# Rope scores over stacked parts, forgetting attention by key block, and separate key and query scales

## The chip, the cores and the metric

The kernel runs on one core of a Trainium2 chip. The metric is the device time of one execution in microseconds (us). Before the change three runs gave 2504.44, 2506.77 and 2509.23 us, median 2506.77. The chip's engines are called by what they do here: TensorE (PE in the rows; its weight loads are PEld), VectorE (DVE), ScalarE (ACT), GpSimd (POOL) and SyncE (SP), which issues the DMAs.

## The reference, cut to what matters

The program computes three transformer blocks over 512 tokens and 1024 features, all in float32. The change touches two attentions. The first is the latent attention of the second block: 8 heads, a query and key of 192 features each, of which 128 carry no position and 64 go through rope; the rope part of the key is one for all heads.

```python
q = (rms_norm(q_lat, q_a_norm) @ w_uq).reshape(B, S, 8, 192)
kv = (rms_norm(kv_lat, kv_a_norm) @ w_ukv).reshape(B, S, 8, 128 + 128)
k = concatenate([k_nope, k_pe], -1)          # k_pe: the same 64 for every head
q = rms_norm(q, q_head_norm); k = rms_norm(k, k_head_norm)
q = concatenate([q[..., :128], rope(q[..., 128:])], -1)   # and k the same
o = causal_softmax_attention(q, k, v, 1 / sqrt(192))
```

The second is the forgetting attention of the third block: 8 heads of 64 features, with a running sum of log forget gates as bias.

```python
for blk in range(4):                          # 128 queries each
    logits = q[q0:q1] @ k[:q1].T * scale + cum[q0:q1, None] - cum[None, :q1]
    p = softmax(where(causal, logits, NEG_INF))
    outs.append(p @ v[:q1])
```

## The kernel before, in words

Everything is held with features (or keys) on the 128 partitions and 512 tokens along the free dimension. A projection splits both operands into a high and a low fp32r part and adds three matmuls (`mm`, lines 429 to 431, 512 columns each; `mm_tok`, lines 439 to 441, 256 columns). Weights come by DMA, 512 KB each, through three raw buffers, are split by ScalarE (line 419) and VectorE (line 420) and lie in two pools of six buffers, `whp` for the high and `wlp` for the low parts. A pool `t` has 53 buffers of 128x512 fp32, and `q` has three for values that live for a few instructions. Of the eight PSUM banks three go to projections (`pm`), two to scores (`sc`), and one each to the roles `tr` (transposes), `po` (value products) and `ms` (everything small: column sums, broadcasts, rope's swap).

The program is written as one list of instructions, and a planner orders them on each engine by priority (the order in which they are written) among those that its own cost model takes to be ready; tiles get a buffer when one is free. So the order on each engine is fixed before the run, and instructions of neighbouring pieces are mixed. `self.fillers` is a list of functions (projections that nobody needs yet), of which one is written after every softmax step by `self.fill()`. `self.later(f, depth)` puts a function in a queue and runs the oldest when more than `depth` are waiting; `flush()` runs the rest, with one filler between two.

Latent attention (`mla`) works on four pairs of heads. For a pair, `kv` makes keys and values and the keys' sums of squares; `q` makes three query tiles (the last has the rope parts of both heads, 64 rows each), their sums of squares into the same PSUM tile, and the rope; `scales` turns all 16 columns of sums into scales with one power on GpSimd (line 572); `keys` broadcasts the keys' scales over partitions (line 1287 in two halves of 64 rows for the rope part, line 584 over 128 rows for each head) and multiplies. The work of the next pair is given as fillers to the loop of the present one. In the loop each head goes through its four query blocks, the widest first: a 128-row fp32 matmul (line 1326), a 64-row fp32 matmul for the rope part (line 1327), the mask (line 1328, bf16), then maximum, exponential and normalization; `apply` transposes the probabilities and multiplies them with the values (line 1304), two steps later.

Forgetting attention (`fox_pair`) also takes pairs of heads, with 64 rows (and 64 output columns) each. Scores of both heads (line 1712) and masks (line 1714) come first, then the softmax; `apply`, one step later, turns the block of each head (line 947, into the one `tr` bank, copied by ScalarE at line 949) and adds the value products by query block and key block (line 1701), 128 columns each:

```python
aT = [self.transposed(p, qb) for p in ps]
for kb in range(qb + 1):
    for par, r in enumerate(ROWS):
        nc.tensor.matmul(po[0][r, qb * P:P * (qb + 1)], vt[...], aT[par][:, kb * P:(kb + 1) * P], start=kb == 0, stop=kb == qb)
```

During the first two pairs the fillers are the other branch's values and the second group's projections, during the last two the other branch's outputs (with a gelu of four VectorE and ScalarE steps each) and four `out_a` projections of twelve matmuls each, which need that branch's norm. After the last pair come `flush()`, `branch_rstd(nb)` (column sums and a power), what is left of the fillers, and `branch("gn_b", ...)`, whose results the next projections need.

Of the kernel before, what the change touches and what calls it, by code (L numbers as in the profile page):

```python
# [286 lines left out]
class Net:  # L287
# [902 lines left out]
    def mla(self, norm, third):  # L1190
# [31 lines left out]
        mulc, addc = self.const([P, 16], F32, "mulc"), self.const([P, 16], F32, "addc")  # L1222
        for j in range(NB):
            kc, qc = slice(4 * j, 4 * j + 2), slice(4 * j + 2, 4 * j + 4)
            nc.vector.memset(mulc[:, kc], 1.0 / 192)
            nc.vector.memset(mulc[:, qc], 1.0)
            nc.vector.tensor_scalar(addc[:, kc], kcol[:, j:j + 1].to_broadcast([P, 2]), 1.0 / 192, EPS, mult, add)
            nc.vector.tensor_scalar(addc[:, qc], vq[:, j:j + 1].to_broadcast([P, 2]), 192 * EPS, None, mult)
# [10 lines left out]
        def pair(c):  # L1239
# [3 lines left out]
            def kv():  # L1243
                w = self.load("w_ukv", c, 1, 512)
                r["sums"], r["k"], r["q"], r["v"] = self.psa("sums"), [], [], []
                for par in range(2):
                    ps = self.psm()
                    self.mm(ps, w, par * P, kvs)
                    y = self.t(F32, "kn")
                    nc.scalar.copy(y, ps)  # L1250
                    sq = self.q(F32, "sq")
                    nc.scalar.activation(sq, ps, AF.Square)
                    self.sums(r["sums"], sq, par, 1, par == 0)
                    r["k"].append(y)
                for tp in range(2):
                    ps = self.psm()
                    for b in range(2):
                        self.mm_tok(ps[:, b * 256:(b + 1) * 256], kvs, 2 * tp + b, w, 256, 256)
                    y = self.t(F32, "mv")
                    nc.vector.tensor_copy(y, ps)  # L1260
                    r["v"].append(y)

            def q():
                w = self.load("w_uq", c, 2, 384)
                for i in (2, 0, 1):
# [6 lines left out]
                    self.sums(r["sums"], sq, 2 + i % 2, 1 + i // 2, False, i < 2)  # L1272
                    r["q"].append(y)
                r["qr"] = self.rope(r["q"].pop(0), self.v("qh_r"), cos, sin)

            def scales():
                m = self.s(16, "ms")
                nc.vector.tensor_tensor(m, r["sums"][:, 0:16], mulc, mult)
                nc.vector.tensor_tensor(m, m, addc, add)
                r["rs"] = self.rpow(m, 16)  # L1280
# [12 lines left out]

            return [kv, q, scales, keys], r
# [18 lines left out]
        for f in (work[0], gates[1], work[1], work[2], gates[2], work[3]):  # L1313
            f()
        for c in range(4):
# [5 lines left out]
            for par in range(2):  # L1321
                rp = slice(64 * par, 64 * par + 64)
                for qb in range(NB - 1, -1, -1):
# [3 lines left out]
                    nc.tensor.matmul(ps[:, :n], cur["qr"][rp, qb * P:n], cur["kr"][rp, :n], start=False, stop=False)  # L1327
# [3 lines left out]
                    sc = cur["rs"][:, 4 * qb + 2 + par:4 * qb + 3 + par]  # L1331
# [357 lines left out]
    def fox_pair(self, q, k, vt, c, cl, cum, out, norm):  # L1689
        nc = self.nc  # L1690
        mult, add = ALU.mult, ALU.add
        po = []

        def apply(ps, qb):
            if not po:
                po.append(self.psa("fxo", "po"))
            aT = [self.transposed(p, qb) for p in ps]
            for kb in range(qb + 1):
                for par, r in enumerate(ROWS):
                    col = (kb % 2) * 256 + (2 * cl + par) * 64  # L1700
                    nc.tensor.matmul(po[0][r, qb * P:P * (qb + 1)], vt[kb // 2][:, col:col + 64], aT[par][:, kb * P:(kb + 1) * P], start=kb == 0, stop=kb == qb)  # L1701
            if qb == 0:
                y = self.t(F32, "fxo")
                nc.vector.tensor_copy(y, po[0])
                out.append(y)
                norm.add(c, y)

        for qb in range(NB - 1, -1, -1):
# [6 lines left out]
            prob = []  # L1715
            for par, ps in enumerate(sc):
                cb = cum[2 * c + par]
                p = self.t(F32, "fxp")
                mx = self.s(4, "mx")
                nc.vector.tensor_tensor_reduce(p[:, :n], ps[:, :n], cb[:, :n], 1.0, 4 * NEG, add, ALU.max, mx[:, 0:1])  # L1720
                nc.vector.tensor_scalar(mx[:, 1:2], mx[:, 0:1], -1.0, None, mult)
                self.last = nc.scalar.activation(p[:, :n], p[:, :n], AF.Exp, bias=mx[:, 1:2], scale=1.0, accum_out=mx[:, 2:3])
                nc.vector.reciprocal(mx[:, 3:4], mx[:, 2:3])
                nc.vector.tensor_scalar(p[:, :n], p[:, :n], mx[:, 3:4], None, mult)
                prob.append(p)
            self.fill()
            self.later(lambda p=prob, qb=qb: apply(p, qb), 1)
# [52 lines left out]
```

## Time and profile before

| what | value |
|---|---|
| runs | 2504.44, 2506.77, 2509.23 us |
| the profiled execution | 2498.9 us, its span 2497.1 us, 31348 instructions |
| mean granted clock of TensorE | 0.988 |
| TensorE busy | 2438.4 us, 98% of the span |
| TensorE weight loads busy | 1994.1 us, 80% |
| VectorE, ScalarE, GpSimd busy | 1313.5, 983.0, 62.7 us |
| projections, lines 429, 430, 431 | 2736 each, 1045.1, 1042.8 and 1040.7 us busy |
| latent attention's scores | about 1274 to 1424 us from the span's start |
| forgetting attention | about 1900 to 2058 us |

Busy time of TensorE counts a matmul from its start to the modelled end of its pipeline, so neighbours overlap and the sum of their durations is more than the time that passes. What one costs is read in the timeline as the distance to the next start. In a row with a count (x4) the length runs from the first start to the last end. A clock of 0.50 is 1.2 GHz, 1.00 is 2.4 GHz.

### The profile page before, as it was taken

What the parts mean: (1) busy time and instruction counts of PE and PEld (TensorE: products, weight loads), DVE (VectorE), ACT (ScalarE), POOL (GpSimd) and SP (SyncE); (2) the same over time, 40 slices, a digit from 0 to 9 for tenths busy, and PEclk for the clock granted to TensorE, in tenths of its full rate; (3) what the DMA queues carried; (4) which work ended last, traced back from release to release, by engine and by line L of the source; (5) the groups of instructions that cost most, each with busy time, mean ns of one, the idle gap of its engine ahead of it and who ended that gap; (6) DMA issues with size and microseconds to landing.
All of it is one profiled execution on the core that took longest, in us unless ns stands there. A gap on an engine that the chain in (4) does not pass through costs nothing. (4 is left out here: it accounts for less than half of the span.)

```text
span 2497.1 us, 31348 instructions
## 1 busy us (share of the span) xinstructions
PE 2438.4 (98%) x12622; PEld 1994.1 (80%) x12622; DVE 1313.5 (53%) x2220; ACT 983.0 (39%) x1575; POOL 62.7 (3%) x62
## 2 busy tenths in 40 slices
PE   8999999999999999999999999999999999999998
PEld 6877788888888787777877798888898768888887
DVE  7536556774775664446555654223365465432333
ACT  5423433442444445655324533222245344322221
POOL 0000000000000000000000000000010001000001
PEclk9999999999999999999999999999999989999999
DMA  5223225433433332222322113233213101323321
GB/s 188 93 90 101 90 97 185 135 123 114 152 119 119 126 109 77 68 81 83 113 71 85 37 66 118 93 101 101 93 54 103 61 26 60 96 93 101 100 87 49
DMA packets 71746, 240.78 MB, mean 96 GB/s; under 512 B 8232, under 2 KB 11184, under 8 KB 71600
## 3 DMA queue, kind: packets, MB, share of 16 engines
q1 hardware_dynamic: 71600, 238.78, 29.1%
q8 instruction: 99, 1.62, 0.3%
q14 instruction: 47, 0.39, 0.0%
HBM read 236.64 MB, written 2.11 MB: 96 GB/s over the span
## 5 line engine op out<-in xcount | busy, mean ns | idle before, releaser
L429 PE MATMUL pm<-hi,wh 128*128 128x512 f32 (+1 forms) x2736 | 1045.1, 383 | 11.1 <-ACT hi L393 7.3
L430 PE MATMUL pm<-lo,wh 128*128 128x512 f32 (+1 forms) x2736 | 1042.8, 381 | 0.0
L431 PE MATMUL pm<-hi,wl 128*128 128x512 f32 (+1 forms) x2736 | 1040.7, 380 | 0.0
L419 ACT CAST wh<-raw 128x1024 fp32r<-128x1024 f32 (+1 forms) x372 | 382.3, 1029 | 827.0 <-PE pm L430 581.5
L420 DVE TENSOR_TENSOR wl<-raw,wh 128x1024 fp32r<-128x1024 f32 (+1 forms) x372 | 445.0, 1196 | 448.8 <-ACT wh L419 422.2
L429 PEld LDWEIGHTS pm<-hi,wh 128*128 128x128 f32 x2736 | 517.2, 189 | 110.9 <-ACT hi L393 8.9
L430 PEld LDWEIGHTS pm<-lo,wh 128*128 128x128 f32 x2736 | 517.0, 189 | 96.5 <-issue 3.8
L431 PEld LDWEIGHTS pm<-hi,wl 128*128 128x128 f32 x2736 | 516.8, 189 | 96.1 <-issue 3.6
L439 PE MATMUL pm<-wh,hi 128*128 128x256 f32 x400 | 116.0, 290 | 4.9 <-ACT vt L816 4.9
L1393 DVE CUSTOM_DVE_ANT_0 adaw<-adaw,cb 128x1024 f32<-128x1024 f32 x72 | 87.9, 1220 | 55.7 <-DMA adaw<-in_w_ada 55.5
L441 PE MATMUL pm<-wh,lo 128*128 128x256 f32 x400 | 115.1, 288 | 0.0
L440 PE MATMUL pm<-wl,hi 128*128 128x256 f32 x400 | 114.2, 286 | 0.0
L1472 DVE TENSOR_TENSOR sg<-sg,pm 128x512 f32<-128x512 f32 x44 | 30.2, 686 | 132.8 <-PE pm L431 132.7
L572 POOL TENSOR_TENSOR rc<-ms,nhalf 128x4 f32<-128x4 f32 (+2 forms) x29 | 38.6, 1333 | 2335.2 <-DVE ms L577 1779.3
L439 PEld LDWEIGHTS pm<-wh,hi 128*128 128x128 f32 x400 | 77.8, 194 | 5.8 <-ACT vt L816 5.3
L441 PEld LDWEIGHTS pm<-wh,lo 128*128 128x128 f32 x400 | 77.8, 194 | 0.5 <-issue 0.3
L440 PEld LDWEIGHTS pm<-wl,hi 128*128 128x128 f32 x400 | 77.8, 194 | 0.5 <-issue 0.2
L481 PE MATMUL pm<-hi,wh 128*128 128x256 f32 (+1 forms) x216 | 61.5, 309 | 9.9 <-ACT hi L400 7.1
L970 DVE SCALAR_TENSOR_TENSOR uy<-ur,vec,uy 128x511 f32<-128x511 f32 x88 | 65.7, 747 | 9.0 <-ACT uy L968 8.0
L258 DVE TENSOR_TENSOR acc<-acc,sq 128x512 f32<-128x512 f32 (+1 forms) x93 | 54.6, 595 | 24.0 <-ACT sq L254 22.8
L482 PE MATMUL pm<-lo,wh 128*128 128x256 f32 (+1 forms) x216 | 66.0, 307 | 0.3 <-DVE lo L1424 0.3
L483 PE MATMUL pm<-hi,wl 128*128 128x256 f32 (+1 forms) x216 | 66.2, 308 | 0.0
(350 smaller groups left out, 2363.7 us busy)
## 6 DMA issues: line engine op xcount, KB each, us to landing
raw<-in_w_gu SPq DMA_DIRECT2D x88, 512.0 KB, 3.3
adaw<-in_w_ada SPq DMA_DIRECT2D x72, 512.0 KB, 3.3
raw<-in_w_dn SPq DMA_DIRECT2D x48, 512.0 KB, 3.3
raw<-in_w_up SPq DMA_DIRECT2D x44, 512.0 KB, 3.3
raw<-in_w_g SPq DMA_DIRECT2D x16, 512.0 KB, 3.3
raw<-in_w_l0qk SPq DMA_DIRECT2D x16, 512.0 KB, 3.4
raw<-in_w_l SPq DMA_DIRECT2D x12, 512.0 KB, 3.3
X<-in_x SPq DMA_DIRECT2D x16, 256.0 KB, 5.6
```

What stands on the lines that cost most here:

```text
L419: nc.scalar.copy(wh[:, :n], raw[:, :n])
L420: nc.vector.tensor_tensor(wl[:, :n], raw[:, :n], wh[:, :n].bitcast(F32), ALU.subtract)
L429: self.nc.tensor.matmul(out, a, xh, start=start and k == 0, stop=False)
L430: self.nc.tensor.matmul(out, a, xl, start=False, stop=False)
L431: self.pe = self.nc.tensor.matmul(out, b, xh, start=False, stop=stop and k == n - 1)
L439: self.nc.tensor.matmul(out, xh[:, sl], a, start=start and k == 0, stop=False)
L440: self.nc.tensor.matmul(out, xh[:, sl], b, start=False, stop=False)
L441: self.pe = self.nc.tensor.matmul(out, xl[:, sl], a, start=False, stop=stop and k == len(x) - 1)
L482: self.nc.tensor.matmul(o[:, sl], wh[:, k], xl[:, sl], start=False, stop=False)
L483: self.nc.tensor.matmul(o[:, sl], wl[:, k], xh[:, sl], start=False, stop=k == 7)
L970: nc.vector.scalar_tensor_tensor(y[:, sh:], raw[:, :S - sh], self.v("fconv_w", 44 * (2 - sh) + f), y[:, sh:], mult, add)
L1393: nc.vector.tensor_tensor_reduce(w, w, cb, 0.5, 0.0, ALU.mult, ALU.add, mod[:, i:i + 1])
```

## The change

In latent attention the rope part of a query is split into a high and a low fp32r part that are stacked, high in the head's own 64 rows and low in the other 64. The rope part of the key, which has the same 64 features in both halves, is scaled with the broadcast over 128 rows and split into a high and a low tile; these lie in one buffer of `whp` or `wlp` for each head. Line 1327 becomes two one-pass matmuls over 128 rows, one with the key's high and one with its low part. The half-height broadcasts of line 1287 are gone. The function `scales` is gone as a step: the keys' scales are made in `kv`, right behind their sums, the queries' in `q`, each with one VectorE instruction and a power of 8 columns.

In forgetting attention the probabilities of all four query blocks of a pair are kept, in five tiles. Four functions per pair go into the queue and are run one per step of the next pair: three turn the key blocks (0; 1 and 3; 2) of both heads, into the `tr` and `ms` banks in turns, one copy of 512 columns per bank; the fourth, `values`, multiplies by key block, with 512, 384, 256 and 128 columns, and stores the result.

```diff
-        mulc, addc = self.const([P, 16], F32, "mulc"), self.const([P, 16], F32, "addc")
+        addk, addq = self.const([P, 8], F32, "addk"), self.const([P, 8], F32, "addq")
...
+        def scales(ps, f, a):
+            m = self.s(8, "ms")
+            nc.vector.scalar_tensor_tensor(by2(m), ps[:, 0:16].rearrange("p (j c) -> p j c", c=4)[:, :, 0:2], f, by2(a), mult, add)
+            return self.rpow(m, 8)
...
-                    self.sums(r["sums"], sq, par, 1, par == 0)
+                    self.sums(sums, sq, par, 1, par == 0, par == 1)
...
+                r["rk"] = scales(sums, 1.0 / 192, addk)
...
+                r["rq"] = scales(sums, 1.0, addq)
+                qr = self.rope(r["q"].pop(0), self.v("qh_r"), cos, sin)
+                r["qr"] = []
+                for own, other in (ROWS, ROWS[::-1]):
+                    y = self.t(F32R, "qs")
+                    nc.scalar.copy(y[own], qr[own])
+                    nc.vector.tensor_tensor(y[other], qr[own], y[own].bitcast(F32), ALU.subtract)
+                    r["qr"].append(y)
...
             def keys():
-                rs = r["rs"]
-                bk = self.psa("pbc")
-                for j in range(NB):
-                    for par in range(2):
-                        nc.tensor.matmul(bk[64 * par:64 * par + 64, j * P:(j + 1) * P], rs[:, 4 * j + par:4 * j + par + 1].to_broadcast([P, 64]), self.ident, start=True, stop=True)
-                r["kr"] = self.t(F32, "krc")
-                nc.vector.tensor_tensor(r["kr"], kr, bk, mult)
+                rk = r["rk"]
+                r["kr"] = []
                 for par in range(2):
-                    b = self.bcast_ps([rs[:, 4 * j + par:4 * j + par + 1] for j in range(NB)])
+                    b = self.bcast_ps([rk[:, 2 * j + par:2 * j + par + 1] for j in range(NB)])
                     nc.vector.scalar_tensor_tensor(r["k"][par], r["k"][par], gqk, b, mult, mult)
+                    y = self.q(F32, "krc")
+                    nc.vector.tensor_tensor(y, kr, b, mult)
+                    w = (self.whp, self.wlp)[par].tile([P, 1024], F32R, tag=("wh", "wl")[par], name="krs")
+                    h, l = w[:, 0:S], w[:, S:2 * S]
+                    nc.scalar.copy(h, y)
+                    nc.vector.tensor_tensor(l, y, h.bitcast(F32), ALU.subtract)
+                    r["kr"].append((h, l))
-            return [kv, q, scales, keys], r
+            return [kv, q, keys], r
...
-                    nc.tensor.matmul(ps[:, :n], cur["qr"][rp, qb * P:n], cur["kr"][rp, :n], start=False, stop=False)
+                    for kr_part in cur["kr"][par]:
+                        nc.tensor.matmul(ps[:, :n], cur["qr"][par][:, qb * P:n], kr_part[:, :n], start=False, stop=False)
...
     def fox_pair(self, q, k, vt, c, cl, cum, out, norm):
+        both = self.t(F32, "fxp")
+        tiles = [[self.t(F32, "fxp") for _ in range(2)] for _ in ROWS]
+        prob = [{3: t[0], 2: t[1][:, 0:3 * P], 0: t[1][:, 3 * P:], 1: both[:, 2 * P * par:2 * P * par + 2 * P]} for par, t in enumerate(tiles)]
+        aT = [{}, {}]
+        def turned(role, blocks):
+            ps, y, o = self.psa("tr", role), self.t(F32, "aT"), 0
+            for par, kb in blocks:
+                aT[par][kb] = y[:, o:o + S - kb * P]
+                for qb in range(kb, NB):
+                    nc.tensor.transpose(ps[:, o:o + P], prob[par][qb][:, kb * P:(kb + 1) * P], self.ident)
+                    o += P
+            nc.scalar.copy(y, ps)
+        def values():
+            po = self.psa("fxo", "po")
+            for kb in range(NB):
                 for par, r in enumerate(ROWS):
                     col = (kb % 2) * 256 + (2 * cl + par) * 64
+                    nc.tensor.matmul(po[r, kb * P:], vt[kb // 2][:, col:col + 64], aT[par][kb], start=kb == 0, stop=kb == NB - 1, skip_group_check=True)
+            y = self.t(F32, "fxo")
...
             self.fill()
-            self.later(lambda p=prob, qb=qb: apply(p, qb), 1)
+            self.step()
+        def turn2(*what):
+            for role, blocks in zip(("tr", "ms"), what):
+                turned(role, blocks)
+        self.queue += [
+            lambda: turn2([(0, 0)], [(1, 0)]),
+            lambda: turn2([(0, 1), (0, 3)], [(1, 1), (1, 3)]),
+            lambda: turn2([(0, 2), (1, 2)]),
+            values,
+        ]
```

## Rows read from the trace of the kernel before

**Rows 1.** The page: busy us, share of the span, instructions; granted clock in 40 slices.
```profile
PE 2438.4 (98%) x12622; PEld 1994.1 (80%) x12622; DVE 1313.5 (53%) x2220; ACT 983.0 (39%) x1575; POOL 62.7 (3%) x62
PEclk9999999999999999999999999999999989999999
```
**Rows 2.** Stretch sum: span, PE PEld DVE ACT POOL busy (count), clock, DMA.
```profile
1274.00:1424.00 150.00, 147.55 (x831) 108.51 (x830) 90.61 (x224) 63.09 (x145) 8.70 (x3) 0.98 0.19 61
```
**Rows 3.** Stretch sum of line 1327 alone: span, PE busy, PEld busy, clock, DMA.
```profile
1274.00:1424.00 150.00, 25.70 (x64) 9.43 (x64) 0.98 0.19 61
```
**Rows 4.** Timeline of TensorE, a score: start us, length us, line, tiles, shape, count.
```profile
1274.13 1.02 PE L1326 MATMUL mls<-kn,qn 128*128 128x512 f32 x2
1275.08 1.12 PE L1327 MATMUL mls<-krc,ropeo 64*128 64x512 f32 x2
1276.14 0.23 PE L1328 MATMUL mls<-bf_mask_q,bf_ident 128*128 128x128 bf16 x1
```
**Rows 5.** Timeline of TensorE: projections and one full-height fp32 matmul.
```profile
1281.00 0.28 PE L441 MATMUL pm<-wh,lo 128*128 128x256 f32 x1
1281.12 0.28 PE L439 MATMUL pm<-wh,hi 128*128 128x256 f32 x1
...
1286.25 0.48 PE L430 MATMUL pm<-lo,wh 128*128 128x512 f32 x1
1286.57 0.39 PE L431 MATMUL pm<-hi,wl 128*128 128x512 f32 x1
1286.80 0.40 PE L429 MATMUL pm<-hi,wh 128*128 128x512 f32 x1
...
1292.41 1.02 PE L1369 MATMUL swap<-qn,cst 128*128 128x512 f32 x2
1293.27 0.61 PE L1304 MATMUL mlo<-aT,mv 128*128 128x128 f32 x4
```
**Rows 6.** Groups by line and shape: busy us, mean ns | idle before, releaser.
```profile
L1287 PE MATMUL pbc<-cst,rc 128*64 128x128 f32 x64 | 4.4, 279 | 1.7 <-POOL rc L572 1.7
...
L572 POOL TENSOR_TENSOR rc<-ms,nhalf 128x16 f32<-128x16 f32 x5 | 14.5, 2901 | 307.9 <-DVE ms L733 167.9 <-DVE ms L1279 140.0
L572 POOL TENSOR_TENSOR rc<-ms,nhalf 128x4 f32<-128x4 f32 x12 | 13.5, 1123 | 1166.5 <-DVE ms L577 930.3 <-DVE mx L1723 102.1 <-DVE mx L928 75.9
```
**Rows 7.** Timeline of VectorE and ScalarE: a product from PSUM, a split.
```profile
1270.24 0.68 DVE L1289 TENSOR_TENSOR krc<-ropeo,pbc 128x512 f32<-128x512 f32 x1
...
2046.63 0.62 ACT L393 CAST hi<-u 128x512 fp32r<-128x512 f32 x1 [2.15 <-DVE u L1606]
...
2047.38 0.68 DVE L394 TENSOR_TENSOR lo<-u,hi 128x512 fp32r<-128x512 f32 x1
```
**Rows 8.** Stretch sums of line 1701 alone, second and last pair, columns as rows 3.
```profile
1939.10:1980.50 41.40, 4.77 (x40) 2.84 (x40) 1.00 0.15 52
2010.20:2058.00 47.80, 8.31 (x52) 4.94 (x52) 0.82 0.07 23
```
**Rows 9.** Timeline of TensorE in stick-breaking, value products and what follows.
```profile
941.60 1.83 PE L1186 MATMUL sbo<-sba,svt 128*64 128x512 f32 x4
943.36 0.59 PE L1150 MATMUL z<-sqk 64*128 64x384 f32 x2
...
959.84 1.52 PE L1186 MATMUL sbo<-sba,svt 128*64 128x384 f32 x12
961.29 0.70 PE L1150 MATMUL z<-sqk 64*128 64x512 f32 x2
```
**Rows 10.** Waits of TensorE: line, releaser, us in total, times, longest.
```profile
PE tr L947 <- ACT aT L949: 3.5, 3, 3.2
```
**Rows 11.** Stretch sums at low clock, columns as rows 2.
```profile
1320.40:1327.30 6.90, 6.90 (x27) 6.14 (x26) 3.53 (x8) 2.58 (x5) 0.00 (x0) 0.51 0.22 76
2030.40:2044.10 13.70, 11.74 (x54) 8.74 (x56) 5.29 (x23) 5.82 (x15) 1.16 (x1) 0.50 0.04 15
```
**Rows 12.** Timeline of TensorE behind the forgetting attention, idle time in brackets.
```profile
2068.32 0.50 PE L429 MATMUL pm<-hi,wh 128*128 128x512 f32 x1 [1.88 <-ACT hi L393]
```

More of the change, by code (lines that the diff above doesn't have):

```diff
@@ L1244, in kv @@
                 w = self.load("w_ukv", c, 1, 512)
-                r["sums"], r["k"], r["q"], r["v"] = self.psa("sums"), [], [], []
+                sums, r["k"], r["q"], r["v"] = self.psa("sums"), [], [], []
                 for par in range(2):
@@ L1263, in q @@
             def q():
-                w = self.load("w_uq", c, 2, 384)
+                w, sums = self.load("w_uq", c, 2, 384), self.psa("sums")
                 for i in (2, 0, 1):
@@ L1271, in q @@
                     nc.scalar.activation(sq, ps, AF.Square)
-                    self.sums(r["sums"], sq, 2 + i % 2, 1 + i // 2, False, i < 2)
+                    self.sums(sums, sq, i % 2, 1 + i // 2, i == 2, i < 2)
                     r["q"].append(y)
[L1274 to L1280, printed above, removed]
@@ L1312, in mla @@
         kr = self.rope(kpe, self.v("kh_r"), cos, sin)
-        for f in (work[0], gates[1], work[1], work[2], gates[2], work[3]):
+        for f in (work[0], gates[1], work[1], gates[2], work[2]):
             f()
@@ L1330, in mla @@
                     nc.vector.tensor_reduce(mx[:, 0:1], ps[:, :n], AX.X, ALU.max)
-                    sc = cur["rs"][:, 4 * qb + 2 + par:4 * qb + 3 + par]
+                    sc = cur["rq"][:, 2 * qb + par:2 * qb + par + 1]
                     nc.vector.tensor_scalar(mx[:, 1:2], mx[:, 0:1], sc, -1.0, mult, mult)
@@ L1691, in fox_pair @@
         mult, add = ALU.mult, ALU.add
[L1692 to L1698, printed above, removed]
+        both = self.t(F32, "fxp")
[13 more added lines that the diff above has]
+            for kb in range(NB):
                 for par, r in enumerate(ROWS):
                     col = (kb % 2) * 256 + (2 * cl + par) * 64
[L1701 to L1706, printed above, removed]
+                    nc.tensor.matmul(po[r, kb * P:], vt[kb // 2][:, col:col + 64], aT[par][kb], start=kb == 0, stop=kb == NB - 1, skip_group_check=True)
+            y = self.t(F32, "fxo")
+            nc.vector.tensor_copy(y, po)
+            out.append(y)
+            norm.add(c, y)
         for qb in range(NB - 1, -1, -1):
@@ L1714, in fox_pair @@
                 nc.tensor.matmul(ps[:, qb * P:n], self.bf["ident"], self.bf["mask_q"], start=False, stop=True)
[L1715 removed]
             for par, ps in enumerate(sc):
                 cb = cum[2 * c + par]
[L1718 removed]
+                p = prob[par][qb]
                 mx = self.s(4, "mx")
[L1720 removed]
+                nc.vector.tensor_tensor_reduce(p, ps[:, :n], cb[:, :n], 1.0, 4 * NEG, add, ALU.max, mx[:, 0:1])
                 nc.vector.tensor_scalar(mx[:, 1:2], mx[:, 0:1], -1.0, None, mult)
[L1722 removed]
+                self.last = nc.scalar.activation(p, p, AF.Exp, bias=mx[:, 1:2], scale=1.0, accum_out=mx[:, 2:3])
                 nc.vector.reciprocal(mx[:, 3:4], mx[:, 2:3])
[L1724 to L1725 removed]
+                nc.vector.tensor_scalar(p, p, mx[:, 3:4], None, mult)
             self.fill()
[L1727 removed]
+            self.step()
[8 more added lines that the diff above has]
+        ]
     def block3(self, x, out):
```

9 lines of the change are left out of this document (3 added, 6 removed).

## The prediction

> **What bounds the kernel now.** I read the page first: TensorE is busy 98% of the span and no other engine passes 53% [rows 1]. A busy TensorE only says that some matmul was in flight, so the next view is the timeline of TensorE, where the distance from one start to the next is what an instruction really costs. In the ordinary projections that distance is 0.23 us for 512 columns and 0.12 us for 256 columns [rows 5] with nothing between, so the stretch is bound by what TensorE has to stream, and fewer or shorter passes are worth their full price as long as fillers keep it fed. The third view is the stretch sums of the latent attention's scores: 147.55 us of 150 busy on TensorE, 90.61 on VectorE, 63.09 on ScalarE [rows 2]. The fourth is the clock and the waits around the forgetting attention: a stretch of 13.7 us ran at 0.50 of the clock [rows 11], and it follows the largest wait of a transpose, 3.2 us for ScalarE's copy of the one bank [rows 10].
>
> **Rope scores, the largest term.** Line 1327 multiplies 64 rows in fp32, which the trace shows as two passes per matmul: 64 instructions, 25.70 us busy in the stretch [rows 3]. Busy counts the pipelined end of each; at 512 columns the row says 1.12 us but the next instruction starts after 1.06 [rows 4], so I scale by 1.06/1.12 and get 24.3 us. After the change there are again 64 instructions (32 score tiles, two parts), each one pass of fp32r over all 128 rows: 0.23 us at 512 columns and 0.12 at 256 [rows 5], 0.175 at 384 by the line between them. At 128 columns no row stands here; below by the same line is 0.06, above is twice the 256-column price if short ones streamed slower, 0.24; I take 0.12, the nearest row. The four widths average 0.161, times 64 is 10.3 (9.4 to 12.2). Gain 14.0, from 12 to 15.
> Two seams. Before line 1327 the 512-column fp32 pair of line 1326 takes 0.95 us to the next start [rows 4], where a pair with full-height neighbours takes 0.86 [rows 5]: 0.09 goes, 32 times, 2.9 us. The Trainium skill (TensorEngine Tiling, Key Properties) says that changing the tiling mode drains the engine; the 0.95 against 0.86 agrees. By that rule alone the seam on the far side of line 1327 would go too, some 3 us that I don't count. Against that, the first one-pass matmul behind an fp32 one starts its successor after 0.32 instead of 0.23 [rows 5]: 0.09, 32 times, 2.9 us. The seams cancel.
>
> **Key scales.** The 64 half-height broadcasts of line 1287 go: 4.4 us busy [rows 6], by the same scaling 4.2; the two full broadcasts per pair stay. TensorE also waited 1.7 us in front of them for GpSimd's power [rows 6], which took 2.90 us for 16 columns and 1.12 for 4; for 8 I put 1.7 between them. It is now two powers per pair, but that for the keys starts after `kv`, a whole `q` (eighteen projection matmuls and the sums) before `keys` needs it, and that for the queries is first read by the next pair's softmax. I take the whole 1.7 (0 to 1.7). Together 5.9.
> What is added: per pair VectorE gets two key products instead of one, two low parts for the keys and two for the queries, five instructions of about 0.68 [rows 7], 3.4 us; ScalarE four copies of 0.62 [rows 7], 2.5 us; VectorE's small ones stay about equal. Over four pairs 13.6 and 9.9 us, which brings VectorE to 104 and ScalarE to 73 in a stretch that shrinks to some 131: covered in sum. For pairs two to four they are issued as fillers several score steps before their first use. VectorE's queue is in order, so a softmax step behind them is late by up to 1.4 us; two score banks and the two steps by which `apply` lags take that up. In the first pair nothing lies between `keys` and the scores: from the broadcast to the scores it was two VectorE products, now key product, rope product, ScalarE copy, low part, about 1.3 us more, against scales that are there earlier. I put 0 (from -2 to +2). The rope parts hold one buffer of each weight pool per pair, two where pairs overlap; four of six are left for some three loads per pair: 0 (to +3).
>
> **Forgetting attention.** The value products: one pair at full clock has 40 instructions with 4.77 us busy [rows 8], in bursts of two to fourteen; scaled for the ends, 4.3. The same columns then go in four double matmuls of 512, 384, 256 and 128 columns, the two heads in the two column halves. Stick-breaking has just this shape: 384, 256 and 128 together took 1.45 us from start to start [rows 9]. Its 512 took 1.76 [rows 9]; two passes with both heads side by side would be the 0.86 of rows 5. The probabilities are here turned a whole step before, for both heads alike, so I take 0.95: 2.4 per pair (2.3 to 3.2). Gain 1.9, four times, 7.6 (4.4 to 8).
> The transposes stay 80 and cost what they did. What goes is the wait for the single bank: 3.5 us [rows 10], since the two tiles of a step now lie in two banks and the copies come a step earlier than their use. Bursts also fall: by the code eight of transposes and four of value products per pair become three and one, and each makes one following projection pay the 0.09 of above: 8 times 0.09, four times, 2.9 (0 to 4).
> The clock: 13.7 us at 0.50 hold 11.74 of work [rows 11], so 5.9 us were lost there. The row in front is the 3.2 us wait. With the wait gone I expect most of it back, but a gelu chain is still in front of the copies on ScalarE: 4 (0 to 6).
> The flush: four steps of the last pair now stand behind the loop instead of one, with one `out_a` filler (twelve matmuls of 0.23, 2.8 us) between each. They cover the copies (about 0.6 each) but are used up when the last column sums come, so the power of `branch_rstd` (1.12 for four columns [rows 6]) and its two hops are now bare, where three fillers stood; then the 1.88 us before the next projections [rows 12] comes as before. Price +2 (0 to +7, if the copies show as well).
>
> **Sum.** 14.0 + 5.9 + 7.6 + 3.5 + 2.9 + 4 - 2 = 36 us off the profiled execution's 2498.9 us (its span is 2497.1, 1.8 lie around it): 2463. The median of the runs shown, 2506.8, is 7.9 above that execution; I forecast for the median, 2470.
>
> **Rivals.**
> A: the softmax chain becomes the bound in latent attention. For it: VectorE at 104 of 131 us with order fixed, ada's reductions in the same queue. Against: TensorE's 147.55 of 150 [rows 2], the score steps pipelined over two banks. Then only a quarter of the 19.9 us there is kept, 5, and the total is 21: 2486.
> B: the forgetting attention gives nothing. For it: heads one after the other as in the 1.76 of rows 9 (gain 4.4 instead of 7.6), the slow clock returns in the flush, all copies bare, and some ten more tiles of the general pool of 53 are alive. Against: the flush still has four fillers. Then 4.4 + 2.9 - 7 is about 0, and 20 remain: 2487.
> C, slower: the clock. It fell to 0.50 in latent attention already once, for 6.9 us [rows 11], among column sums and short score tiles; the change thins TensorE's work exactly there and packs transposes together. Each microsecond at half clock gives back half of one, so it decides from 72 us of slow clock on; if the scores' whole 130 us ran so, +65 - 36 is 2536. Against: 143 of the 150 us are at full clock with the same transposes among them. [...]
>
> **Numbers.** Forecast 0.70, A 0.12, B 0.12, C 0.03, and 0.03 for both A and B together (about no change). The forecast's own bounds, summed unevenly, are 28 to 46 us: 2461 to 2479; executions of one kernel here spread by 5 us and the profiled one lay 6 below the lowest, so I widen to 2452, and up to 2492 for A and B. This measurement can tell 0.2%, 5 us, from no change: faster 0.90 (forecast, A and most of B), same 0.06, slower 0.04.
>
> **What would show it.** Right: line 1327's successors at 0.23 us from start to start at 512 columns and a sum near 10 us; no half-height broadcasts; the stretch of latent attention's scores near 131 us; value products in runs of sixteen with about 2.4 us per pair; no transpose waiting for a copy by more than 0.5 us; full clock around the end of the third pair. Wrong: gaps of TensorE before line 1326 that end on VectorE or ScalarE (A); value products 1.7 us for 512 columns, or gaps between turn steps in the flush (B); a slow clock in the scores (C).

## The result, and the profile after

The changed kernel takes 2479.22 us (median of 4 runs, 2476.49 to 2481.86), the kernel before on the same chip 2505.61 (4 runs, 2501.52 to 2509.23): a ratio of 0.9895, interval 0.9876 to 0.9914, 26.4 us less. Forecast were 2470 and 36 us less; the time lies within the range, 9 us above the forecast. The profiled execution took 2479.63 us, with a span of 2477.8; the forecast put it at 2463, and it is 19.3 us under the profiled execution before.

The page after (rows as [rows 1]):
```profile
PE 2414.9 (97%) x12462; PEld 1987.4 (80%) x12462; DVE 1325.0 (53%) x2232; ACT 990.7 (40%) x1579; POOL 65.7 (3%) x66
PEclk9999999999999999999999999999999998999999
```
TensorE is busy 23.5 us less, VectorE 11.5 and ScalarE 7.7 more. Where the time went is read from landmarks that both kernels have. From the last value product of stick-breaking to the last score of latent attention it was 254.3 us and is 246.4: 8.0 off where 19.9 were forecast. From the forgetting attention's first score to the first projection of 512 columns that needs its second normalization it was 168.4 and is 151.2: 17.2 off where 16.0 were forecast. What lies outside is 5.8 us longer in this pair of executions; its work is the same in both, and such parts differ by some us between any two executions here (stick-breaking's last value product starts between 1156.7 and 1163.1 us in the fourteen profiles of this document).

The scores of latent attention, all engines and then line 1337 alone, which answers to line 1327 (columns as [rows 2] and [rows 3]; the stretch ends as far behind the last score as there):
```profile
1273.80:1418.90 145.10, 137.45 (x795) 110.36 (x796) 103.93 (x246) 72.31 (x160) 9.82 (x6) 0.94 0.22 70
```
```profile
1273.80:1418.90 145.10, 19.86 (x64) 10.60 (x64) 0.94 0.22 70
```
VectorE with 103.93 and ScalarE with 72.31 us stand where the prediction had them (104 and 73). TensorE has lost 10 us of work, but of 145.10 us it is now idle for 7.65, where 2.45 of 150 were [rows 2], and the granted clock is 0.94 instead of 0.98. The prediction put this stretch near 131 us.

The passes themselves, a score of 384 columns: first of the kernel before, then after (start, length, line; the distance from start to start counts):
```profile
1304.21 0.81 PE L1326 MATMUL mls<-kn,qn 128*128 128x384 f32 x2
1304.95 0.91 PE L1327 MATMUL mls<-krc,ropeo 64*128 64x384 f32 x2
1305.79 0.38 PE L1304 MATMUL mlo<-aT,mv 128*128 128x128 f32 x1
```
```profile
1277.30 0.81 PE L1335 MATMUL mls<-kn,qn 128*128 128x384 f32 x2
1277.65 0.81 PE L1337 MATMUL mls<-krs,qs 128*128 128x384 f32 x2
1278.30 0.23 PE L1338 MATMUL mls<-bf_mask_q,bf_ident 128*128 128x128 bf16 x1
```
Before, 0.74 and 0.84 us; after, 0.35 and 0.65. The first one-pass matmul starts 0.03 us behind the start of the last fp32 pass already and then holds its successor for 0.47, so the seam that [rows 5] seemed to price at 0.09 costs nothing: 1.00 us is just two fp32 passes of 0.325 and two single ones of 0.175 (what such passes take in this trace in front of one of their own kind and in front of the mask).

The waits of TensorE in the scores (in us in total, times, longest), before and then after:
```profile
PE pbc L1287 <- POOL rc L572: 1.7, 2, 1.4
PE mls L1326 <- ACT p L1334: 0.7, 2, 0.4
PE bc L584 <- DVE kn L1292: 0.7, 1, 0.7
```
```profile
PE bc L584 <- DVE ropea L1381: 2.8, 3, 0.9
PE mls L1335 <- ACT p L1344: 2.0, 4, 0.6
PE mlo L1314 <- ACT aT L949: 1.8, 3, 1.1
PE mls L1335 <- DVE kn L1294: 0.8, 1, 0.8
PE swap L1379 <- DVE ms L1230: 0.7, 3, 0.3
```
The wait for GpSimd's power [rows 6] is gone. In its place stands one for VectorE's product with the rope's swap, once at each of the second to fourth pairs, and waits for ScalarE, 3.8 us where 0.7 were. The timeline of all engines around the first of them:
```profile
1291.70 1.49 PE L1379 MATMUL swap<-qn,cst 128*128 128x512 f32 x2 [0.26 <-DVE ms L1230]
1291.79 1.64 POOL L572 TENSOR_TENSOR rc<-ms,nhalf 128x8 f32<-128x8 f32 x1 [5.78 <-DVE ms L1230]
...
1293.30 0.69 DVE L1381 TENSOR_TENSOR ropea<-swap,sin 128x512 f32<-128x512 f32 x1 [0.87 <-PE swap L1379]
1294.02 0.69 DVE L1384 TENSOR_TENSOR ropeo<-ropeo,ropea 128x512 f32<-128x512 f32 x1
...
1294.13 2.05 PE L584 MATMUL bc<-cst,rc 128*128 128x128 f32 x8 [0.94 <-DVE ropea L1381]
1294.75 1.26 ACT L1285 CAST qs<-ropeo 64x512 fp32r<-64x512 f32 x2 [4.41 <-DVE ropeo L1384]
1296.03 0.56 ACT L1344 ACTIVATE p<-mls,mx,rc 128x256 f32<-128x256 f32 x1
...
1296.74 2.08 PE L1335 MATMUL mls<-kn,qn 128*128 128x512 f32 x2 [0.56 <-ACT p L1344]
```
The swap and the keys' broadcast both take the one bank of the role `ms`. Before, GpSimd's power of 16 columns lay between them; now the keys' power is long done, the broadcast stands right behind the swap in TensorE's order, and it waits until VectorE has read the bank. Behind it the second thing is seen: ScalarE's two new copies of the queries' rope parts stand in front of a softmax's exponential (1296.03), for which the next score waits. And TensorE's clock fell around each of the three places, at the first of them 0.9 us before the wait for the bank began (1292.30 and 1293.19 us). Stretch sums at low clock, columns as [rows 11], the first three in latent attention, the fourth in the flush of the forgetting attention:
```profile
1292.30:1302.50 10.20, 8.70 (x31) 6.51 (x30) 6.35 (x13) 4.90 (x10) 1.13 (x1) 0.50 0.00 0
1336.70:1340.10 3.40, 2.90 (x8) 1.55 (x8) 2.72 (x8) 3.08 (x8) 0.00 (x0) 0.50 0.02 5
1374.30:1377.70 3.40, 3.03 (x14) 2.64 (x13) 2.02 (x4) 2.01 (x4) 0.00 (x0) 0.50 0.00 0
2019.40:2026.20 6.80, 5.43 (x17) 4.66 (x18) 6.60 (x14) 3.64 (x8) 0.00 (x0) 0.50 0.00 0
```
That is 17 us at 1.2 GHz in the scores, where 6.9 were [rows 11]. In the forgetting attention the 13.7 us of [rows 11] shrink to 6.8; a second slow stretch, at its second normalization, grows from 3.4 to 6.8.

The value products of its last pair, all sixteen in one run (as [rows 8]), and the waits of its whole stretch (as [rows 10]):
```profile
2033.95 2.38 PE L1725 MATMUL fxo<-aT,fvt 128*64 128x512 f32 x16
2036.25 0.50 PE L429 MATMUL pm<-hi,wh 128*128 128x512 f32 x1
```
```profile
PE bc L584 <- POOL rc L572: 3.1, 2, 1.7
PE tr L1716 <- DVE fxp L1746: 1.8, 1, 1.8
PE fxs L1735 <- DVE mx L1742: 0.5, 1, 0.5
```
From start to start the run takes 2.30 us. The 3.2 us wait for the transposes' bank is gone; the two waits of 1.4 and 1.7 us for GpSimd's powers and the 1.8 us for the last probabilities are the flush's. The 1.88 us of [rows 12] shrink to 0.5.

### The profile page after: what moved, and what is told of

Read it like the earlier page. It is cut to its first block, busy times and chain, and to the rows that moved or that the text cites. A ratio compares the mean times of both kernels' runs of the same rounds, so it can differ in the third digit from the quotient of the medians.

```text
span 2477.8 us, 31023 instructions
## 1 busy us (share of the span) xinstructions
PE 2414.9 (97%) x12462; PEld 1987.4 (80%) x12462; DVE 1325.0 (53%) x2232; ACT 990.7 (40%) x1579; POOL 65.7 (3%) x66
## 5 line engine op out<-in xcount | busy, mean ns | idle before, releaser
L572 POOL TENSOR_TENSOR rc<-ms,nhalf 128x4 f32<-128x4 f32 (+3 forms) x33 | 40.8, 1237 | 2315.1 <-DVE ms L577 1871.0
```

## The experiments

Theory 1: latent attention's work on TensorE shrank as forecast, and the new order gave half of it back, by the shared bank and the slow clock around it. Theory 2 (the prediction's rival A): the parts' copies and differences bind the scores.

All runs, each against the kernel before on its own chip. "Latent" is the distance from the last value product of stick-breaking to the first broadcast of the forgetting attention's cumulative sums, in the profiled execution (it holds the output projection and all that is moved there); "slow" is the time at 1.2 GHz from the first to the last latent score; "forgetting" is the distance named above. "Clock" is the median granted clock of all runs of the row, and "full clock" an estimate from it: how far the median of span times clock, the time that would be left at 2.4 GHz throughout, lies under that of the kernel before on the same chip. A clock is recorded to 0.001, which is 2.5 us, so 2 us between two of these estimates say nothing.

| kernel | median us | ratio (interval) | latent | slow | forgetting | clock | full clock |
|---|---|---|---|---|---|---|---|
| before | | | 722.4 | 6.8 | 168.4 | 0.987 | 0 |
| changed | 2479.22 | 0.9895 (0.9876 to 0.9914) | 714.1 | 17.1 | 151.2 | 0.985 | |
| a0_after, the changed again | 2479.83 | 0.9909 (0.9891 to 0.9927) | 715.6 | 17.1 | 151.9 | 0.985 | 27.0 |
| e1_mla_only | 2495.57 | 0.9978 (0.9968 to 0.9988) | 718.3 | 27.3 | 168.9 | 0.9835 | 15.6 |
| e2_fox_only | 2481.88 | 0.9925 (0.9909 to 0.9941) | 720.9 | 3.4 | 151.4 | 0.9895 | 13.8 |
| e3_swap_pm | 2470.47 | 0.9871 (0.9854 to 0.9888) | 708.5 | 6.8 | 151.3 | 0.988 | 28.4 |
| e4_gate_between | 2474.91 | 0.9885 (0.9867 to 0.9903) | 711.5 | 6.8 | 150.9 | 0.988 | 26.1 |
| e5_both | 2470.71 | 0.9879 (0.9858 to 0.9899) | 707.4 | 3.4 | 151.1 | 0.988 | 27.2 |
| e6_scales_only | 2482.13 | 0.9923 (0.9903 to 0.9942) | 718.2 | 10.2 | 151.5 | 0.988 | 17.4 |
| e7_one_power | 2479.89 | 0.9912 (0.9895 to 0.993) | 715.0 | 13.7 | 151.4 | 0.9845 | 27.2 |
| e8_norm_early | 2477.88 | 0.9905 (0.9889 to 0.9922) | 711.3 | 13.7 | 155.1 | 0.985 | 27.4 |
| e9_norm_early2 | 2475.43 | 0.9899 (0.9883 to 0.9915) | 710.9 | 13.7 | 152.2 | 0.986 | 28.8 |
| e10_copies_pool | 2473.48 | 0.9893 (0.9874 to 0.9911) | 713.5 | 10.2 | 151.5 | 0.9895 | 22.5 |
| e11_parts_later | 2467.76 | 0.9867 (0.9851 to 0.9884) | 707.5 | 6.8 | 151.3 | 0.989 | 29.7 |

The same latent code stands in the changed kernel, a0 and e1, with 17.1, 17.1 and 27.3 us of slow clock, and in e3, e8 and e9, with 6.8, 13.7 and 13.7: of one execution's clock some 10 us at half speed, 5 us of time, are chance. The clock over all runs is steadier: 0.984 to 0.985 in the ten of the changed kernel and a0, 0.988 to 0.990 in e3's four. And at full clock all versions with stacked parts and with the copies on ScalarE lie together, 26 to 30 us under the kernel before (a0, e3, e4, e5, e7, e8, e9 and e11): the 12 us of time between a0 and e11 are for the most part TensorE's clock.

**The two halves apart.** e1 has the changed latent attention and the old `fox_pair`, e2 the reverse:
```diff
 # e1
-        self.queue += [
-            lambda: turn2([(0, 0)], [(1, 0)]),
-            lambda: turn2([(0, 1), (0, 3)], [(1, 1), (1, 3)]),
-            lambda: turn2([(0, 2), (1, 2)]),
-            values,
-        ]
+            self.later(lambda p=prob, qb=qb: apply(p, qb), 1)
...
 # e2
-                    for kr_part in cur["kr"][par]:
-                        nc.tensor.matmul(ps[:, :n], cur["qr"][par][:, qb * P:n], kr_part[:, :n], start=False, stop=False)
+                    nc.tensor.matmul(ps[:, :n], cur["qr"][rp, qb * P:n], cur["kr"][rp, :n], start=False, stop=False)
```


> The latent attention as changed, the forgetting attention as before. The comparison of the two traces puts 7 us of the gain in latent attention (from the end of stick-breaking to its output projections 301.4 us before, 294.8 changed) and 15 in the forgetting attention. If the stages add, this kernel is 5 to 10 us faster than before (0.996 to 0.998 of it). If latent attention is worth the 20 us of the prediction and one execution hid it, 0.992. In its trace the three waits of 0.95 us in front of the keys' broadcasts stand again, and the clock is again at half for 10 to 17 us of the scores.

> The forgetting attention as changed, the latent attention as before. If the stages add: 13 to 18 us faster than before, 0.993 to 0.995. If the gain in the forgetting attention was only a clock that happened to fall elsewhere, under 8 us, over 0.997.


Measured: e1 5.4 us under the kernel before (2500.96 there), e2 19.1. The forgetting attention is worth what was forecast or a little more; what is missing is missing in latent attention. At full clock e1 lies 15.6 us under the kernel before and e2 13.8: the change of latent attention took some 10 us back by a lower clock, that of the forgetting attention gained some 5 by a higher one.

**The shared bank.** e3 gives the rope's swap one of the projections' three banks:
```diff
-        ps = self.psa("swap")
+        ps = self.psm("swap")
```


> The changed kernel with rope's swap in one of the three projection banks instead of the one bank for small things. Theory of the bank: in the changed order the keys' broadcast stands right behind the swap and waits 0.95 us, three times, until VectorE has read it; here the three waits go (2.8 us, and some of the waits of scores behind them), and if the half clock came from these holes another 3 to 8 us: 2470 to 2476 where the changed kernel has 2479. Theory of the busy VectorE and ScalarE (the added splits bind the softmax): the waits move to the scores and the time stays within 2 us of the changed kernel. Theory of the thin work (clock falls because scores, sums and transposes are short, holes or not): waits go, half clock stays above 12 us, 2476.


Measured: 30.5 us under the kernel before. The same place in e3:
```profile
1283.79 1.02 PE L1379 MATMUL swap<-qn,cst 128*128 128x512 f32 x2
...
1287.35 1.13 PE L584 MATMUL bc<-cst,rc 128*128 128x128 f32 x8
...
1287.84 1.26 ACT L1285 CAST qs<-ropeo 64x512 fp32r<-64x512 f32 x2 [2.46 <-DVE ropeo L1384]
...
1289.12 0.56 ACT L1344 ACTIVATE p<-mls,mx,rc 128x256 f32<-128x256 f32 x1
...
1289.83 1.13 PE L1335 MATMUL mls<-kn,qn 128*128 128x512 f32 x2 [1.35 <-ACT p L1344]
```
The broadcast no longer waits, the slow clock is back at 6.8 us, and "latent" is 5.6 us shorter than in the changed kernel. The medians of e3 and the changed kernel lie 9 us apart, on different chips; the ratio intervals of e3 and a0 don't overlap. Their profiles differ by 13.9, of which 5.6 lie where the edit is and as much in work ahead of it that is the same in both, so the profiles show 5 to 6 us for the bank. All of it is clock: from the first to the last score it is 5.0 us less, with 10.3 us less at half speed, which is 5.1 us of time. Over all runs it is the same, a clock of 0.988 instead of 0.985 and no difference at full clock. For the waits only moved: that for ScalarE's copies has grown from 0.56 to 1.35 us, since TensorE now comes there earlier.

How the wait for the bank and the clock hang together is not shown. The first fall in the changed kernel came before the wait, and e8 and e9, with e3's latent code, have 13.7 us of slow clock in their one profile, which is what the thin work of e3's expectation would have. Against the thin work stands the clock of all of e3's runs, with the same short matmuls.

**Other work between the two users of the bank.** e4 puts a gate projection between the fillers `q` and `keys`, e5 does this beside e3's bank:
```diff
-                self.fillers += work
-            self.fillers += [gates[3:4], gates[4:5], [], [idle] * 4 + [gates[5]] + [idle] * 3 + gates[6:]][c]
+                self.fillers += work[:2] + gates[3 + c:4 + c] + work[2:]
+            else:
+                self.fillers += [idle] * 4 + [gates[6]] + [idle] * 3 + gates[7:]
```


> The changed kernel with one gate projection (24 matmuls of 0.23 us) written between the queries' work and the keys' broadcasts in each of the first three pairs, instead of behind them. Theory of the bank: the three waits of 0.95 us go as well, 2.8 us. Theory of the thin work: 5.5 us of dense projections now stand right where the clock fell, so the half clock shrinks below 7 us and 5 us more come back: 2471. Theory of the busy VectorE and ScalarE: no change, 2479, as the same work is on their queues.

> Swap in another bank and a gate projection between the fillers, together. Theory 1 (the missing gain is the shared bank's three waits of 0.945 us and the half clock they start; each edit alone cures the clock, so the clock is gained once): about what the swap's bank alone gave, 2467 to 2472. Theory 2 (two separate losses, one per edit): the gains add, 2462 to 2466. If the moved gates only shift TensorE's work around: 2472 to 2478.


Measured: e4 26.1 us under the kernel before, slow clock at 6.8 us; e5 29.5, which is e3 again. The two edits cure the same loss, as theory 1 has it. By itself e4 would fit the thin work as well, since dense projections now stand where the clock fell. In e4 one transposes' copy on ScalarE comes 2.4 us late, so the order cures one wait and makes another.

**Each part of the change alone.** e6 undoes the stacking (one fp32 product of 64 rows per score, scales apart), e7 the two powers (one of 16 columns behind the queries' sums, parts stacked):
```diff
 # e6
-                    for kr_part in cur["kr"][par]:
-                        nc.tensor.matmul(ps[:, :n], cur["qr"][par][:, qb * P:n], kr_part[:, :n], start=False, stop=False)
+                    rp = ROWS[par]
+                    nc.tensor.matmul(ps[:, :n], cur["qr"][rp, qb * P:n], cur["kr"][rp, :n], start=False, stop=False)
 # e7
-                r["rq"] = scales(sums, 1.0, addq)
+                scales(r["m"][:, 8:16], sums, 1.0, addq)
+                m = self.rpow(r["m"], 16)
+                r["rk"], r["rq"] = m[:, 0:8], m[:, 8:16]
```


> The changed kernel itself, so that the variants of this call have it on their own chip: 22 to 28 us under the kernel before by either theory.

> The changed kernel with the rope scores again one fp32 product of 64 rows per score tile, one rope tile of keys per pair; scales apart and the new forgetting attention stay. Theory 1 (the stacked parts bring what their instructions show, 10 us from start to start, and losses elsewhere hide it): 8 to 12 us slower than the changed kernel. Theory 2 (the parts' copies and differences on ScalarE and VectorE hold the scores up and eat the gain): within 4 us of the changed kernel.

> The changed kernel with one power of 16 columns behind the queries' sums again, for keys and queries together; stacked parts stay. If scales apart are worth what the forecast put on them (1.7 us of wait for GpSimd): 1 to 4 us slower than the changed kernel. If what they do is to put the swap and the keys' broadcast next to each other in the one bank: the three waits of 0.945 us go, a wait for the power takes their place at the first pair alone, and the time is 0 to 6 us under the changed kernel.


Measured: a0 20.4 us under the kernel before; e6 2.3 above a0, e7 level with it. By its bound of 4 us e6 speaks for theory 2, but it ran at a clock of 0.988 and a0 at 0.985: at full clock it is 9.6 us above a0, as theory 1 has it (8 to 12). By its waits it does not decide: without the stacking the scores have hardly a wait left,
```profile
PE mls L1323 <- ACT p L1332: 1.7, 1, 1.7
```
so the stacked parts give TensorE 15 us less work in the scores and their neighbours (summed as below) and lose 8 of it, 6 to waits and 2 to the clock, as both theories say; e3 and e11 tell what those waits are. Against e2, which differs from e6 by the scales apart and the half-height broadcasts alone, "latent" is 2.7 us shorter with 6.8 us more slow clock. e7 has three waits too, of 1.9 us each, now for GpSimd:
```profile
PE bc L584 <- POOL rc L572: 5.7, 3, 1.9
```
Neither of its expectations came: with the two powers the change put a wait of 0.94 us in the place of one of 1.9 at the second to fourth pairs, and the time is level, with 13.7 us of slow clock where a0 has 17.1.

**ScalarE's copies.** e10 (on e3) moves the queries' two copies to GpSimd:
```diff
-                    nc.scalar.copy(y[own], qr[own])
+                    nc.gpsimd.tensor_copy(y[own], qr[own])
```


> Swap in another bank, and the queries' two half-height copies on GpSimd instead of ScalarE. Rival A of the prediction in a local form (ScalarE's order: two copies of 0.62 us stand in front of a softmax's exponential, and TensorE waits 1.35, 0.5 and 0.9 us for it): those waits go and the scores' 6.8 us of slow clock with them, 2 to 6 us under 2470.5. If the softmax chain has slack anywhere else or GpSimd holds VectorE up: within 1.5 us of 2470.5 or above.


Measured: 28.2 us under the kernel before, 3 us worse than e3, and 6 at full clock. The timeline where e3 waited 1.35 us:
```profile
1288.97 2.01 POOL L572 TENSOR_TENSOR rc<-ms,nhalf 128x8 f32<-128x8 f32 x1 [6.23 <-DVE ms L1230]
...
1290.93 1.80 POOL L1285 CAST qs<-ropeo 64x512 fp32r<-64x512 f32 x2
1291.57 0.68 DVE L1286 TENSOR_TENSOR qs<-ropeo,qs 64x512 fp32r<-64x512 f32 x1 [1.55 <-POOL qs L1285]
1292.77 0.69 DVE L1286 TENSOR_TENSOR qs<-ropeo,qs 64x512 fp32r<-64x512 f32 x1 [0.51 <-POOL qs L1285]
1293.48 0.21 DVE L1342 TENSOR_SCALAR mx<-mx,rc 128x1 f32<-128x1 f32 x1
1293.79 0.56 ACT L1344 ACTIVATE p<-mls,mx,rc 128x256 f32<-128x256 f32 x1 [6.73 <-DVE mx L1342]
...
1294.50 2.07 PE L1335 MATMUL mls<-kn,qn 128*128 128x512 f32 x2 [4.34 <-ACT p L1344]
```
The copies stand behind the power on GpSimd, VectorE's differences wait for the copies, and a softmax's 0.2 us step stands behind them in VectorE's queue: 4.34 us. A miss as a remedy, it shows the mechanism: not how much the engines have to do (ScalarE has less here), but what stands in front of a softmax step in an in-order queue.

e11 (on e3) leaves the copies on ScalarE and makes the queries' parts a filler of their own, a score step behind `keys`:
```diff
-                qr = self.rope(r["q"].pop(0), self.v("qh_r"), cos, sin)
+                r["ro"] = self.rope(r["q"].pop(0), self.v("qh_r"), cos, sin)
...
+            def parts():
+                qr, r["qr"] = r["ro"], []
...
-            return [kv, q, keys], r
+            return [kv, q, keys, parts], r
...
```
For the first pair, where no loop runs yet, `parts` stands in front of `keys`.


> Swap in another bank, and the queries' rope parts (two copies on ScalarE, two differences on VectorE) made a score step after the keys instead of straight behind the rope. Theory (in the in-order queues of ScalarE and VectorE the copies stand in front of an exponential or of a transposes' copy, and wait there for the rope's sum): the waits of the scores for the probabilities and of the value products for the transposes' copy at the second and third pair, some 4.5 us together in the kernel with the swap's bank alone, go; 2464 to 2468. Rival (the waits come from how much ScalarE and VectorE have to do there, not from where it stands, or the slow clock returns elsewhere): 2469 to 2474.


Measured: 32.2 us under the kernel before. The waits of its scores, first those of e3 (both to 1410 us):
```profile
PE mls L1335 <- ACT p L1344: 3.1, 4, 1.3
PE mlo L1314 <- ACT aT L949: 2.4, 3, 1.0
```
```profile
PE mls L1336 <- ACT p L1345: 1.9, 4, 0.8
PE pm L431 <- DVE wl L420: 1.0, 2, 0.5
PE mls L1336 <- DVE kn L1295: 0.8, 1, 0.8
```
The waits for `p` and `aT` fall from 5.5 to 1.9 us, 3.6 of the 4.5 expected; 1.0 us for weights is new. Of the time this is 1 us in "latent", and 0.9867 against e3's 0.9871 is no difference that these intervals can tell; at full clock the two are level as well (29.7 and 28.4 us). So theory 1 holds for the larger part, and theory 2 names waits that are there, but whose end gains nothing clear of the noise. e11 is the lowest version run; that it beats e3 is not shown, that it beats the changed kernel is (2466.69 to 2469.71 against 2475.76 to 2481.86 in all runs of the changed one).

**The flush of the forgetting attention.** e8 (on e3) drops the idle steps between the last pairs' fillers, so that the first branch's power and normalization come some score steps earlier; e9 also holds one projection piece back:
```diff
-                self.fillers = [gates[0], idle, gates[1], idle, *gates[2:]]
+                self.fillers = [*gates, idle]
 # e9, behind the four out_a fillers
+                self.fillers.insert(-1, idle)
```


> Swap in another bank, and in the forgetting attention the first branch's power and normalization two and three score steps earlier, so that the first projection piece of the output stands ahead of the last pair's transposes. If the 1.43 us wait for GpSimd's power, the 1.77 us wait for the last probabilities and half of the 6.8 us of slow clock behind them are what the flush costs: 3 to 6 us under the kernel with the swap's bank alone (2470.5), 2464 to 2468. If the normalization's sixteen instructions on VectorE and ScalarE, now among the last pair's softmax, hold the scores up instead: within 2 us of it or slower.

> The same, and the last projection piece held back until behind the value products, in front of the second branch's sums. If VectorE's copy of the value products and the square are bare otherwise: 1 to 2 us under the run with the normalization early. If other matmuls already cover them: the same within 1 us, or 1 us slower because the transposes' copy before it is bare.


Measured: e8 23.8 us under the kernel before, e9 26.2. "Forgetting" is 3.7 us longer than in e3 for e8 and 0.8 for e9; the rest of their distance to e3 lies outside it, where the code is the same, and at full clock there is none beyond the estimate's error. In e8 the waits of 1.4 and 1.8 us go, but others come; around 1997 us in e8:
```profile
1996.74 0.69 DVE L1596 SCALAR_TENSOR_TENSOR u<-ge,pm 128x512 f32<-128x512 f32 x1 [0.70 <-ACT ge L1512]
1997.35 0.68 DVE L1727 COPY fxo<-fxo 128x512 f32<-128x512 f32 x1
1997.95 0.68 DVE L1605 SCALAR_TENSOR_TENSOR u<-u,gt 128x512 f32<-128x512 f32 x1
1998.55 0.68 DVE L1742 CUSTOM_DVE_ANT_0 fxp<-fxs,cumb 128x512 f32<-128x512 f32 x1
...
1999.29 1.65 PE L1735 MATMUL fxs<-fqk 64*128 64x384 f32 x2 [2.43 <-DVE mx L1742]
```
The last pair's first score step stands on VectorE behind the other branch's products, and 13.7 us at 1.2 GHz follow. The expectation named the normalization; it is the products of the gates ahead of it, packed by the missing idle steps. In e9 the same wait stands.

## Why the prediction was right, and where it was not

Summed over TensorE's matmuls in the two profiled executions, each by its distance to the next start, with the waits and the time lost at 1.2 GHz (half of it) set apart:

| us | forecast | measured |
|---|---|---|
| rope parts, the scores beside them, transposes, value products, masks | -14.0 | -15.5 |
| keys' broadcasts | -4.2 | -3.5 |
| waits of TensorE | -1.7 | +4.9 |
| slow clock | 0 | +5.5 |
| other matmuls | 0 | +0.6 |
| latent attention | -19.9 | -8.0 |
| value products | -7.6 | -5.1 |
| transposes, scores and others, bursts | -2.9 | -6.2 |
| waits | -3.5 + 2 | -2.1 |
| slow clock | -4 | -3.9 |
| forgetting attention | -16.0 | -17.2 |

**Rope scores: right in sum, by other steps.** The 64 passes fell from 23.6 to 14.2 us, 9.4 and not 14.0: the first of two after an fp32 pass books the seam to itself. The other 6.1 came off the neighbours. The forecast counted 2.9 of this, set 2.9 against it for the change of type, and left the far seam out. No run shows a price for the change of type. The Trainium skill (TensorEngine Tiling (Array Packing), Key Properties) says that changing the tiling mode drains the engine: in front of line 1327 the trace agrees, with 0.74 us against 0.65. For the 0.84 against 0.65 in it that is not enough: its two passes take 0.43 and 0.41 us where a full-height one takes 0.325, and behind the first of them the mode does not change.

**Key scales: the step that failed.** The broadcasts' matmuls went as priced. But "I take the whole 1.7" asked only when the keys' power is ready, not what the broadcast stands behind once it is: the rope's swap, in the same single bank. Three waits of 0.94 us took the place of the power's 1.4 and 0.3. Without them (e3) the clock of all runs is higher, and other waits stand in their place.

**"A softmax step behind them is late by up to 1.4 us; two score banks and the two steps take that up": wrong in size.** What is late is ScalarE's exponential, behind 1.26 us of copies, in a queue that the sentence left out, and the cover was not there: scores and value products wait 3.8 us for ScalarE, 3.1 more than before. That is rival A's mechanism with a price of some 3 us of waits, not the 15 of its case; e11 takes most of these waits away by position alone.

**The clock.** Rival C had the place and the direction; its price here is 5.5 us, as the slow stretches stayed near the three waits and did not spread over the scores. The forecast gave this 0 within the likeliest case, which was too little: over all runs e1's clock is 0.9835 where the kernel before has 0.987, an estimated 9 us.

**Forgetting attention: right.** 17.2 for 16.0, 19.1 by e2's medians. Value products: 2.30 us in the last pair, for the 2.4 forecast, but 11.6 over four pairs instead of 9.6, since at the second and third the runs of sixteen are broken up by transposes and scores. The bursts gave more than priced, if all that came off the neighbours is theirs. The bank's wait went, and the clock gave 3.9 of the 4 us back, with 6.8 us of slow clock left in the flush. The flush cost two bare powers and a wait for the last probabilities, 4.9 us, of which the shorter wait before the next projections gave 1.4 back.

**The sum.** The two distances fell by 8.0 and 17.2, 25.2 together; e1 and e2 add up to 24.5; the two medians differ by 26.4, a0's by 20.4. The shortfall against 36 is latent attention's 12: 6.6 of waits and 5.5 of clock. Over all runs it is clock for the larger part: at full clock a0 lies 27 us under the kernel before, where the forecast without its 4 for the clock had 32. The 26.4 us are less than the 28 of the forecast's own lower bound; the time is inside the range because that was widened for the spread of executions and for the rivals.

**The signs.** Seen were successors of line 1327 at 0.23 us, no half-height broadcasts, the run of sixteen at 2.30 us and no transpose waiting for a copy. Not seen were a sum near 10 us (14.2) and a stretch of scores near 131 us (145.1); two signs of being wrong came, waits of the scores for ScalarE (A) and a slow clock (C).

Open: how much of latent attention's slow clock each wait starts. It moved by 10 us between executions of the same code, no run here holds it fixed, and at the first place the clock fell before the wait.

## What to carry to other kernels

When a wait goes, look up what now stands next to what in each engine's order, and whether two neighbours share a single buffer: what lay between them, here a wait for another engine, was their cover. Added copies that are "hidden in sum" are priced by what stands behind them in the in-order queue at the step where they are issued; in a step of their own later in the loop they hold less up (5.5 us of waits became 1.9). A stretch in which TensorE is thinned needs a term for its clock even if it was mostly at full clock before, and versions that differ by a few us are compared by the clock of all their runs before a wait is blamed.

## What the runs showed of the hardware

A one-pass fp32r matmul behind an fp32 one costs nothing extra from start to start: at 384 columns 0.35 and 0.65 us, together the 1.00 of their passes apart. A pass over 64 rows costs about 0.1 us more than over 128 at the same columns (0.84 against 0.65 for two of 384). GpSimd's power of 8 columns took 1.64 to 2.01 us. Around waits of 0.9 us in a stretch of short matmuls and column sums TensorE ran at 1.2 GHz for 3.4 to 10.2 us, and the fall came before the wait or behind it; with the swap in another bank the mean clock of the whole program was 0.988 to 0.990 instead of 0.984 to 0.985.
